# Two retention heads' values in seven half-size products instead of eight, in a TensorE-bound block

## The chip, the cores and the metric

The kernel runs on one core of a Trainium2 chip. The metric is the device time of one execution in microseconds (us). Inside the core, TensorE (PE in the profile, PEld for its weight loads) multiplies, VectorE (DVE) and ScalarE (ACT) do elementwise work, GpSimd (POOL) does small work and issues the DMAs of one queue, and SyncE (SP) issues the loads of the weights.

## The reference

Two layers of a block on 512 frames of width 1024. The part that matters here is the retention branch: one combined projection of the normalised input gives, among others, for each of four heads q and k (256 columns each), the values v (512 columns) and the gate g (512 columns).

```python
z = h @ w_in[i] + b_in[i]
_, _, mv, mo, mi, mf, rq, rk, rv, rg, gm, gr = split_cols(z)
...
hr = retention_chunkwise(to_chunks(rq4...), to_chunks(rk4...), to_chunks(rv.astype(f32), R_HEADS), log_gamma)
y_r = (jax.nn.silu(rg.astype(f32)) * head_layernorm(hr, r_norm_g[i], R_HEADS)).astype(dt)
merged = jax.nn.sigmoid(gm) * (y_m @ w_bm[i]) + jax.nn.sigmoid(gr) * (y_r @ w_br[i])
```

Everything is computed to float32 accuracy: each operand is split into a high and a low part (type fp32r), and each product is made of three matmuls, high·high, high·low and low·high.

## The kernel before, in words

**Units of weights.** All weights pass through the core once, as a written list of units (`unit_list`). A `T8` unit holds 1024 rows by 128 columns, gives one 128x512 output tile with the weights as the stationary operand, and takes 24 matmuls with 512 moving columns. A `V` unit holds 256 rows by 512 columns; four of them (`values`, L608 on) give the values of one head with the activations stationary and the weights moving, 96 matmuls of 512 columns. A `PAIR` unit gives two output tiles (256 columns) by a seven-product scheme (Winograd's form of Strassen's): quarters of the activations and sums of quarters (`sevenfold`, `xs`) times quarters of the weights B11, B12, B21, B22 and their sums t1 = B12+B11, t3 = B12+B22, t2 = t1+B22 and t4 = t2+B21 (the second output tile is carried with its sign turned, so all four are additions). That is 84 matmuls of 256 columns (`run_pair`, L421 to L423) instead of 48 of 512. Its last product P4 is put off (`later`) and run by `flush` inside the next unit.

**How a unit's weights come in.** SP loads each piece into one of four `wr` buffers (`fill_raws`, L341 and L343). ScalarE copies it into the high part and VectorE subtracts to get the low part (`split`, L263 and L264). Three such split pieces of 128x1024 are held at a time (`PIECES`). A `PAIR` has pieces A, B, C of 128x1024 (two blocks each) and D of 128x512 (t4). Loads and splits keep the order of the list; splits are asked for two pieces ahead (`LOOK`).

**The weight sums.** t1, t2, t3, t4 of each group of pairs are made in DRAM by DMAs that POOL issues: for each sum one copy and one accumulating copy of 1 MB (0.5 MB in the group `gm`), 8 steps a group, 20 groups, 160 steps (`step`, L307). `due(k)` gives the unit before which step k is issued; it also waits for the last matmul written so far. A group's steps are all issued before its first load.

**Order around the change.** In each layer: mLSTM heads, then `rv_vals(0)`, four tiles of the mLSTM output product, q and k of head 0, gates and four more tiles, then per head scores, attend, values and `r_out` (the gate projection as two pairs, and sixteen transposes, `back`). Values of head 1 come after attend of head 0, those of head 2 after q and k of head 2, those of head 3 after the eight `br` tiles. The framework's scheduler may interleave independent instructions of an engine; tiles of a tag (six `tmp` tiles, `qk`, `v`, eight PSUM banks) are handed out as they come free.

Of the kernel before, what the change touches and what calls it, by code (L numbers as in the profile page):

```python
# [35 lines left out]
F32 = mybir.dt.float32  # L36
# [58 lines left out]
MADE = {"t1": ("B12", "B11"), "t3": ("B12", "B22"), "t2": ("t1", "B22"), "t4": ("t2", "B21")}  # L95

READY = {"P1": 2, "P4": 2, "P5": 3, "P2": 4, "P6": 4, "P3": 4, "P7": 5}


def due(k):  # L100

    return 3 + 5 * min(k, 20) // 4 + 7 * max(k - 20, 0) // 4


def groups():


    g = {}
    for i in range(L):
# [12 lines left out]
        for b in range(4):  # L122
            g[i, f"ff{b}"] = [("w_ff2", b * 1024, 256 * p) for p in range(4)]
    return g


def unit_list(i):

    u = [("IF",)]

    def t8(w, col, row=0):
        u.append(("T8", w, row, col))

# [72 lines left out]
    pairs(ff_order()[0])  # L206
    u.append(("PE", 0))
    u.append(("PE", 1))
    pairs(ff_order()[1])
    full("w_pe_gate")  # L210
    return u


def build(ctx, tc, ins, out):
# [27 lines left out]
    br_dram = tc.dram_tile([L, KT, P, T], F32, name="br_spill")  # L242
    gm_dram = tc.dram_tile([L, 4, P, T], F32, name="gm_spill")
    bm_dram = tc.dram_tile([L, KT, P, T], F32, name="bm_spill")


    bc = cpool.tile([P, L, NB], F32, name="bc")
# [22 lines left out]
        cur[kind] = new  # L270


    index, given, sums, k = {}, {}, {}, 0
    for g, v in groups().items():
        index[g] = len(index)
        for x in GIVEN:
            given[g, x] = ins["wpairs"][k:k + len(v)]
            k += len(v)
        for x in MADE:
            sums[g, x] = tc.dram_tile([len(v), P, Q], F32, name=f"s{index[g]}{x}")  # L280

    def block(g, x):
        return given[g, x] if x in GIVEN else sums[g, x]
# [4 lines left out]
    def sum_steps():  # L288

        first = lambda g: [(g, "t1", 0), (g, "t3", 0), (g, "t1", 1), (g, "t3", 1)]  # L290
        second = lambda g: [(g, "t2", 0), (g, "t2", 1), (g, "t4", 0), (g, "t4", 1)]
        gs = list(index)
        out = first(gs[0])
        for a, b in zip(gs, gs[1:]):
            for x, y in zip(second(a), first(b)):
                out += [x, y]
        return out + second(gs[-1])

    steps = sum_steps()
# [2 lines left out]
    def step():  # L302
# [5 lines left out]

        tc.add_manual_dep(dma.ins, cur["mm"].ins.name, SYNC, reason="pace of the sums")

    def next_unit():
        n = at["unit"]
        at["unit"] += 1
        while at["step"] < len(steps) and due(at["step"]) <= n:
            step()
        return n


    order = [(n, x) for n, u in enumerate(units) for x in (PIECE if u[0] == "PAIR" else (0,))]
    place = {x: k for k, x in enumerate(order)}  # L320
    raws, pieces = {}, {}

    room = unit_list(0).index(("T8", "w_out", 0, 0))
    cur["room"], cur["more"] = (), None
    at = {"unit": 0, "prep": 0, "load": 0, "whole": 0, "step": 0}

    def fill_raws(most=RAWS + 1):
        while at["load"] < len(order) and len(raws) < most:
            n, x = order[at["load"]]
# [6 lines left out]
            raws[n, x] = r = r or wpool.tile([P, UN], F32, name=f"wr{at['load']}", tag="wr", bufs=RAWS)  # L336
            if x:
                _, g, p = units[n]
                assert made[g] == 8, (g, made[g], at["unit"])
                for k, y in enumerate(PIECE[x]):  # L340
                    in_order("load", nc.sync.dma_start(r[:, k * Q:(k + 1) * Q], block(g, y)[p]))  # L341
            else:
                in_order("load", nc.sync.dma_start(r, ins["wstream"][at["whole"]]))  # L343
                at["whole"] += 1
            at["load"] += 1

    def prep_next():
        n, x = order[at["prep"]]
        at["prep"] += 1
        fill_raws()  # L350

        w = Q if x == "D" else UN
        pl = cur["last"] if n >= NU - LAST else wpool
        kw = {"tag": "d", "bufs": 2} if x == "D" else {"tag": "l", "bufs": 2 * LAST} if pl is not wpool else {
            "tag": "w", "bufs": 2 * PIECES}
        out_ = [pl.tile([P, w], F32R, name=f"w{a}{n}_{x}", **kw) for a in "hl"]
# [45 lines left out]
    def run_pair(name, act, done):  # L402
# [31 lines left out]
        for x in ("P6", "P2", "P3", "P7"):  # L434
            product(x)
        later.append(last)

    def pair_tiles(name, act, consume, y=None):

# [350 lines left out]
    for i in range(L):  # L790
# [163 lines left out]
            head_scale(nm, num, 512, mv, hv)  # L954
            return num

        def r_out(h, num, y):
            nm = f"l{i}r{h}o"
            gs = {}

            def gates(w):
                def consume(g):
                    for d in range(2):
                        ac.activation(g[d], g[d], AF.Silu, bias=bcol(i, "brg", 4 * h + 2 * w + d), scale=SIGN[d])
                        gs[2 * w + d] = g[d]

                return consume

            for w in range(2):
                pair_tiles(f"{nm}{w}", xs, gates(w))  # L970
            for v in range(4):
                o = back(nm, num, v)
                if v == 0:
# [36 lines left out]
        def mv_vals(pr, act, rc, mid=None):  # L1010
            return values(i, f"l{i}m{pr}", act, rc, bias_rows(pr * 512), 2, mid)

        def rv_vals(h, mid=None):
# [93 lines left out]
        num = r_attend(2, pt, vv)  # L1107
        qk = r_qk(3)
        for c in range(KT):
# [231 lines left out]
    cur["last"].release()  # L1341
    n3_pool.release()
    x_pool.release()
    assert at["unit"] == NU and at["prep"] == len(order) and not pieces and not raws and at["load"] == len(order) and at["step"] == len(steps)

def _pack_units(a):
# [7 lines left out]
    for i in range(L):  # L1356
        for u in unit_list(i):
            if u[0] == "T8":
                _, nm, r, c = u
                put(a[nm][i, r:r + D, c:c + P])  # L1360
            elif u[0] == "PAIR":
                continue
            elif u[0] == "V":
                _, k, c = u
# [11 lines left out]

def _pack_pairs(a):

    out = []
    for (i, _), g in groups().items():  # L1380
# [3 lines left out]
    return np.ascontiguousarray(np.concatenate(out))  # L1384


def _pack_vecs(a):
# [70 lines left out]
```

## Time and profile before

| what | value |
|---|---|
| median of 3 runs | 2363.36 us (2362.84 to 2367.16) |
| span of the profiled execution | 2361.2 us |
| TensorE, matmuls | 2339.5 us busy, 13788 instructions |
| VectorE | 1579.5 us, 67% |
| ScalarE | 1194.3 us, 51% |
| GpSimd | 262.1 us, 11% |

The profile gives the profiled execution no time of its own beside the span; the runs lie 1.6 to 6.0 us above that span. Matmuls overlap in the pipeline, so one that is shown 389 ns long is followed by the next after about 227 ns: what a matmul costs is read from the distance between starts, not from its length.

### The profile page before, as it was taken

To read this page: it belongs to the slowest core of one execution; us is meant where nothing else is said; L and a number is where in the kernel's file an instruction comes from. 1 tells how busy PE (TensorE), PEld (TensorE's weight loads), DVE (VectorE), ACT (ScalarE), POOL (GpSimd) and SP (SyncE) were. 2 spreads that over 40 slices of the span, in tenths; PEclk is the share of its full clock that TensorE was granted. 3 is DMA by queue.
4 is the path that set the end of the run, shared out by engine and by line. 5 is a ranking of instruction groups with operands and counts; after the bars stand their busy time and mean duration, and the time that the engine had idled before them with its cause. 6 is when DMAs were issued, how large, how long until landed. Compare 5 with 4: busy or idle time off the path is not lost. (4 is left out here: it accounts for less than half of the span.)

```text
span 2361.2 us, 35588 instructions
## 1 busy us (share of the span) xinstructions
PE 2339.5 (99%) x13788; PEld 2074.1 (88%) x13788; DVE 1579.5 (67%) x2435; ACT 1194.3 (51%) x1736; POOL 262.1 (11%) x380
## 2 busy tenths in 40 slices
PE   9999999999999999999999999999999999999998
PEld 7888898998998898899888888999989988998997
DVE  6877566764665676667778675676737656676675
ACT  5755344553553545445457563444526445455454
POOL 4121100000001100001321111000000020000012
PEclk9999999999999999999999999999999999999999
DMA  7766876768688777777776668776786894543441
GB/s 243 196 187 183 232 240 193 206 191 243 190 263 278 213 232 209 216 227 196 201 212 169 191 179 235 233 197 200 189 253 186 274 265 118 166 140 118 154 153 53
DMA packets 177576, 473.49 MB, mean 201 GB/s; under 512 B 17520, under 2 KB 19952, under 8 KB 177408
## 3 DMA queue, kind: packets, MB, share of 16 engines
q1 hardware_dynamic: 118512, 280.25, 35.3%
q0 software_dynamic: 41472, 159.39, 29.1%
q10 hardware_dynamic: 17424, 31.59, 3.7%
q8 instruction: 108, 1.77, 0.3%
q14 instruction: 60, 0.49, 0.1%
HBM read 456.48 MB, written 174.06 MB: 267 GB/s over the span
## 5 line engine op out<-in xcount | busy, mean ns | idle before, releaser
L263 ACT ACTIVATE wh<-wr 128x1024 fp32r<-128x1024 f32 x254 | 268.1, 1057 | 386.7 <-issue 55.2
L264 DVE TENSOR_TENSOR wl<-wr,wh 128x1024 fp32r<-128x1024 f32 x254 | 311.1, 1225 | 148.0 <-ACT wh L263 143.1
L263 ACT ACTIVATE wh_C<-wr 128x1024 fp32r<-128x1024 f32 x76 | 80.5, 1059 | 132.6 <-PE l0bm L373 13.1
L263 ACT ACTIVATE wh_B<-wr 128x1024 fp32r<-128x1024 f32 x76 | 80.4, 1058 | 85.3 <-PE l1bm L373 5.8
L264 DVE TENSOR_TENSOR wl_B<-wr,wh_B 128x1024 fp32r<-128x1024 f32 x76 | 93.9, 1235 | 43.7 <-ACT wh_B L263 43.2
L263 ACT ACTIVATE wh_A<-wr 128x1024 fp32r<-128x1024 f32 x76 | 80.1, 1055 | 76.6 <-PE l1f L373 11.3
L264 DVE TENSOR_TENSOR wl_A<-wr,wh_A 128x1024 fp32r<-128x1024 f32 x76 | 92.9, 1222 | 32.6 <-ACT wh_A L263 31.1
L264 DVE TENSOR_TENSOR wl_C<-wr,wh_C 128x1024 fp32r<-128x1024 f32 x76 | 92.8, 1221 | 29.0 <-ACT wh_C L263 29.0
L372 PE MATMUL l1f<-l1n2h,wh 128*128 128x512 f32 x256 | 99.8, 390 | 0.0
L372 PE MATMUL l0f<-l0n2h,wh 128*128 128x512 f32 x256 | 99.8, 390 | 0.0
L374 PE MATMUL l0f<-l0n2h,wl 128*128 128x512 f32 x256 | 99.7, 389 | 0.0
L374 PE MATMUL l1f<-l1n2h,wl 128*128 128x512 f32 x256 | 99.6, 389 | 0.0
L373 PE MATMUL l1f<-l1n2l,wh 128*128 128x512 f32 x256 | 99.6, 389 | 0.0
L373 PE MATMUL l0f<-l0n2l,wh 128*128 128x512 f32 x256 | 99.6, 389 | 0.0
L263 ACT ACTIVATE wh_D<-wr 128x512 fp32r<-128x512 f32 x76 | 47.6, 627 | 86.0 <-issue 5.3
L264 DVE TENSOR_TENSOR wl_D<-wr,wh_D 128x512 fp32r<-128x512 f32 x76 | 52.1, 686 | 46.3 <-ACT wh_D L263 43.9
L374 PEld LDWEIGHTS l1f<-l1n2h,wl 128*128 128x128 f32 x256 | 48.1, 188 | 10.1
L374 PEld LDWEIGHTS l0f<-l0n2h,wl 128*128 128x128 f32 x256 | 48.0, 188 | 10.0
L373 PEld LDWEIGHTS l0f<-l0n2l,wh 128*128 128x128 f32 x256 | 48.1, 188 | 9.8
L373 PEld LDWEIGHTS l1f<-l1n2l,wh 128*128 128x128 f32 x256 | 48.1, 188 | 9.8
L372 PEld LDWEIGHTS l0f<-l0n2h,wh 128*128 128x128 f32 x256 | 48.1, 188 | 9.8
L372 PEld LDWEIGHTS l1f<-l1n2h,wh 128*128 128x128 f32 x256 | 48.1, 188 | 9.8
(5492 smaller groups left out, 8236.2 us busy)
## 6 DMA issues: line engine op xcount, KB each, us to landing
wr<-wstream SPq DMA_DIRECT2D x254, 512.0 KB, 4.8
wr<-wpairs SPq DMA_DIRECT2D x228, 256.0 KB, 3.7
s0t<-wpairs POOLq DMA_DIRECT2D x6, 1024.0 KB, 8.2
s2t<-wpairs POOLq DMA_DIRECT2D x6, 1024.0 KB, 9.3
s3t<-wpairs POOLq DMA_DIRECT2D x6, 1024.0 KB, 9.0
s4t<-wpairs POOLq DMA_DIRECT2D x6, 1024.0 KB, 9.4
s5t<-wpairs POOLq DMA_DIRECT2D x6, 1024.0 KB, 9.7
s6t<-wpairs POOLq DMA_DIRECT2D x6, 1024.0 KB, 9.0
```

What stands on the lines that cost most here:

```text
L263: a = ac.activation(hi_ap, src, AF.Copy)
L264: return a, ve.tensor_sub(lo_ap, src, hi_ap.bitcast(F32))
L372: te.matmul(o, sh, mh, start=first, stop=False)
L373: te.matmul(o, sh, ml, start=False, stop=False)
L374: cur["mm"] = te.matmul(o, sl, mh, start=False, stop=last)
```

## The change

The values of two retention heads (1024 columns) become one `WIDE` unit. It uses the seven-product scheme with the activation quarters as stationary operand (`xs`, in halves of 128 frames) and weight blocks of 512 rows by 512 columns as moving operand, 512 columns wide. Two WIDE units a layer replace sixteen V units. Each WIDE has 14 pieces (seven blocks in two halves), and counts as seven ticks of the pace of the sums. Seven results per frame tile are combined by VectorE out of PSUM; the first head's values are split at once, the second head's are written to DRAM (`rv_spill`, ScalarE's queue) and read back and split later (`rv_load`).

For the pairs, t4 is no longer made in DRAM and loaded: after piece B (B21 and t2) is split, VectorE adds its two halves in the `wr` buffer, which stays taken until D is split from it. The WIDE groups have eight sum steps, pair groups six. `due` is changed.

The values of heads 2 and 3 are computed before q and k of head 2, not after; the first gate pair of heads 0 and 1 (`r_gates(h, 0)`) runs ahead of the scores of the next head.

```diff
+WIDE = (("P1", "B11", 0), ("P5", "t1", 4), ("P6", "t2", 5), ("P2", "B21", 2), ("P7", "t3", 3), ("P3", "B22", 6),
+        ("P4", "t4", 1))
-PIECE = {"A": ("B11", "t1"), "B": ("B21", "t2"), "C": ("B22", "t3"), "D": ("t4",)}
+PIECE = {"A": ("B11", "t1"), "B": ("B21", "t2"), "C": ("B22", "t3"), "D": ()}
 def due(k):
-    return 3 + 5 * min(k, 20) // 4 + 7 * max(k - 20, 0) // 4
+    return 3 + 6 * min(k, 60) // 4 + 7 * max(k - 60, 0) // 4
...
+        g[i, "rv0"] = [("w_in", 0, CRV)]
+        g[i, "rv2"] = [("w_in", 0, CRV + 1024)]
...
-    v(CRV)
+    u.append(("WIDE", (i, "rv0"), 0))
...
-    v(CRV + 512)
     rg(0)
+    u.append(("WIDE", (i, "rv2"), 0))
     rqk(2)
-    v(CRV + 1024)
     rg(1)
     rqk(3)
     full("w_br")
-    v(CRV + 1536)
...
     (prep_next)
-        r = raws.pop((n, x))
+        r = raws.pop((n, "B" if x == "D" else x))
         in_order("prep", *split(r[:, :w], *out_))
         pieces[n, x] = out_
+        if x == "B":
+            ve.tensor_tensor(r[:, :Q], r[:, :Q], r[:, Q:], OP.add)
+            raws[n, x] = r
...
+    def run_wide(name, act, done, mid=None):
+        n = next_unit()
+        bank = {}
+        for at_, (x, y, j) in enumerate(WIDE):
+            if at_:
+                tick()
+            if x == "P6":
+                flush()
+            if x == "P2" and mid:
+                mid()
+            b = {"P2": "b", "P5": "c", "P3": "c"}.get(x, "a")
+            first = x in ("P1", "P2", "P5")
+            if first:
+                bank[b] = [ps(f"{name}{b}{t}") for t in range(2)]
+            for k in range(4):
+                if k % 2 == 0:
+                    ready(place[n, (y, k // 2)] + LOOK)
+                    wh, wl = pieces.pop((n, (y, k // 2)))
+                h, l = act[k](j)
+                s = slice(k % 2 * T, (k % 2 + 1) * T)
+                f, e = first and k == 0, k == 3
+                for t in range(2):
+                    ts = slice(t * P, (t + 1) * P)
+                    o = bank[b][t]
+                    te.matmul(o, h[:, ts], wh[:, s], start=f, stop=False, skip_group_check=True)
+                    te.matmul(o, h[:, ts], wl[:, s], start=False, stop=False, skip_group_check=True)
+                    cur["mm"] = te.matmul(o, l[:, ts], wh[:, s], start=False, stop=e, skip_group_check=True)
+            for t in range(2):
+                done(x, t, bank[b][t])
...
         def rv_vals(h, mid=None):
-            return values(i, f"l{i}r{h}", xn, None, bias_rows(1024 + h * 512), 1, mid)
+            nm = f"l{i}r{h}"
+            bv = [tmp(f"{nm}bv{d}") for d in range(2)]
+            for d in range(2):
+                nc.sync.dma_start(bv[d], bias_rows(1024 + (h + d) * 512))
+            y = [[cur["low"].tile([P, T], F32, name=f"{nm}y{d}{j}", tag="qk" + "hl"[d], bufs=4) for j in range(NT)]
+                 for d in range(2)]
+            v = value_tiles(nm)
+            def head0(j):
+                split(y[0][j], v[0][j][:, :T], v[1][j][:, :T])
+            def head1(j):
+                nc.scalar.dma_start(rv_dram[i, h // 2, j], y[1][j])
+            def done(x, t, o):
+                a, b = t, 2 + t
+                if x == "P1":
+                    ve.tensor_tensor(y[0][b], o, bv[0], OP.add)
+                elif x == "P2":
+                    ve.tensor_tensor(y[0][b], o, y[0][b], OP.add)
+                    head0(b)
...
+            run_wide(f"{nm}v", xs, done, mid)
+            return v
+        def rv_load(h):
+            v = value_tiles(f"l{i}r{h}")
+            for j in range(NT):
+                t = tmp(f"l{i}r{h}vr{j}")
+                nc.scalar.dma_start(t, rv_dram[i, h // 2, j])
+                split(t, v[0][j][:, :T], v[1][j][:, :T])
+            return v
...
         num = r_attend(0, pt, vv)
-        vv = rv_vals(1)
+        gs = {}
+        r_gates(0, 0, gs)
+        vv = rv_load(1)
         pt = r_scores(1, qk)
         yr = acts(cur["br"], f"l{i}yr0")
-        r_out(0, num, yr)
+        r_out(0, num, yr, gs)
         num = r_attend(1, pt, vv)
+        vv = rv_vals(2)
         qk = r_qk(2)
-        vv = rv_vals(2)
+        gs = {}
+        r_gates(1, 0, gs)
         pt = r_scores(2, qk)
-        r_out(1, num, yr)
+        r_out(1, num, yr, gs)
...
-        vv = rv_vals(3)
+        vv = rv_load(3)
```

More of the change, by code (lines that the diff above doesn't have):

```diff
@@ L270, in in_order @@
         cur[kind] = new
-    index, given, sums, k = {}, {}, {}, 0
+    index, given, sums = {}, {}, {}
+    at = {"unit": 0, "tick": 0, "prep": 0, "load": 0, "whole": 0, "step": 0, "wpairs": 0, "wwide": 0}
     for g, v in groups().items():
         index[g] = len(index)
+        src, n, w = ("wwide", 2, UN) if is_wide(g) else ("wpairs", len(v), Q)
         for x in GIVEN:
-            given[g, x] = ins["wpairs"][k:k + len(v)]
-            k += len(v)
+            given[g, x] = ins[src][at[src]:at[src] + n]
+            at[src] += n
         for x in MADE:
-            sums[g, x] = tc.dram_tile([len(v), P, Q], F32, name=f"s{index[g]}{x}")
+            if x != "t4" or is_wide(g):
+                sums[g, x] = tc.dram_tile([n, P, w], F32, name=f"s{index[g]}{x}")
     def block(g, x):
@@ L294, in sum_steps @@
         for a, b in zip(gs, gs[1:]):
-            for x, y in zip(second(a), first(b)):
-                out += [x, y]
+            s, f = second(a), first(b)
+            while s or f:
+                out += s[:1] + f[:4 // len(second(a)) if len(s) > 1 else 4]
+                f = f[4 // len(second(a)) if len(s) > 1 else 4:]
+                s = s[1:]
         return out + second(gs[-1])
@@ L309, in step, with tick @@
         tc.add_manual_dep(dma.ins, cur["mm"].ins.name, SYNC, reason="pace of the sums")
+    def tick():
+        while at["step"] < len(steps) and due(at["step"]) <= at["tick"]:
+            step()
+        at["tick"] += 1
     def next_unit():
@@ L313, in next_unit @@
         at["unit"] += 1
-        while at["step"] < len(steps) and due(at["step"]) <= n:
-            step()
+        tick()
         return n
-    order = [(n, x) for n, u in enumerate(units) for x in (PIECE if u[0] == "PAIR" else (0,))]
+    order = [(n, x) for n, u in enumerate(units) for x in parts_of(u)]
     place = {x: k for k, x in enumerate(order)}
+    loads = [(n, x) for n, x in order if x != "D"]
     raws, pieces = {}, {}
@@ L324, in build @@
     cur["room"], cur["more"] = (), None
-    at = {"unit": 0, "prep": 0, "load": 0, "whole": 0, "step": 0}
     def fill_raws(most=RAWS + 1):
-        while at["load"] < len(order) and len(raws) < most:
-            n, x = order[at["load"]]
+        while at["load"] < len(loads) and len(raws) < most:
+            n, x = loads[at["load"]]
             r = None
@@ L955, in r_attend, with r_gates, consume, r_out @@
             return num
-        def r_out(h, num, y):
-            nm = f"l{i}r{h}o"
[L959 to L970, printed above, removed]
+        def r_gates(h, w, gs):
+            def consume(g):
+                for d in range(2):
+                    ac.activation(g[d], g[d], AF.Silu, bias=bcol(i, "brg", 4 * h + 2 * w + d), scale=SIGN[d])
+                    gs[2 * w + d] = g[d]
+            pair_tiles(f"l{i}r{h}o{w}", xs, consume)
+        def r_out(h, num, y, gs=None):
+            nm = f"l{i}r{h}o"
+            if gs is None:
+                gs = {}
+                r_gates(h, 0, gs)
+            r_gates(h, 1, gs)
             for v in range(4):
@@ L1343, in build @@
     x_pool.release()
-    assert at["unit"] == NU and at["prep"] == len(order) and not pieces and not raws and at["load"] == len(order) and at["step"] == len(steps)
+    assert at["unit"] == NU and at["prep"] == len(order) and not pieces and not raws and at["load"] == len(loads) and at["step"] == len(steps)
 def _pack_units(a):
@@ L1360, in _pack_units @@
                 put(a[nm][i, r:r + D, c:c + P])
-            elif u[0] == "PAIR":
+            elif u[0] in ("PAIR", "WIDE"):
                 continue
@@ L1377, in _pack_pairs @@
 def _pack_pairs(a):
-    out = []
-    for (i, _), g in groups().items():
+    out, wide = [], []
+    for (i, nm), g in groups().items():
+        if is_wide((i, nm)):
+            (n, r, c), = g
+            w = a[n][i, r:r + D, c:c + 2 * T].reshape(2, 2, 2, P, 2, T)
+            b = {(k, m): w[:, :, k, :, m].transpose(0, 2, 1, 3).reshape(2, P, UN) for k in range(2) for m in range(2)}
+            wide += [b[int(x[1]) - 1, int(x[2]) - 1] for x in GIVEN]
+            continue
         w = np.stack([a[n][i, r:r + D, c:c + 2 * P].reshape(4, 2, P, 2, P) for n, r, c in g])
```

48 lines of the change are left out of this document (41 added, 7 removed).

## The prediction

> **What bounds the kernel now.** I read the page first, then the waits of TensorE, then single tiles for the distance between matmuls, then stretches where the change puts its work.
>
> ```profile
> span 2361.2 us, 35588 instructions
> ...
> PE 2339.5 (99%) x13788; PEld 2074.1 (88%) x13788; DVE 1579.5 (67%) x2435; ACT 1194.3 (51%) x1736; POOL 262.1 (11%) x380
> ...
> q1 hardware_dynamic: 118512, 280.25, 35.3%
> q0 software_dynamic: 41472, 159.39, 29.1%
> q10 hardware_dynamic: 17424, 31.59, 3.7%
> ...
> L263 ACT ACTIVATE wh<-wr 128x1024 fp32r<-128x1024 f32 x254 | 268.1, 1057 | 386.7 <-issue 55.2
> L264 DVE TENSOR_TENSOR wl<-wr,wh 128x1024 fp32r<-128x1024 f32 x254 | 311.1, 1225 | 148.0 <-ACT wh L263 143.1
> ...
> L264 DVE TENSOR_TENSOR wl_D<-wr,wh_D 128x512 fp32r<-128x512 f32 x76 | 52.1, 686 | 46.3 <-ACT wh_D L263 43.9
> ...
> wr<-wstream SPq DMA_DIRECT2D x254, 512.0 KB, 4.8
> ```
> ```profile
> PE l1bgm L374 <- DVE wl L264: 2.0, 1, 2.0
> PE l0o33a L421 <- DVE l0x L1211: 1.6, 1, 1.6
> PE l1o33a L421 <- DVE l1x L1211: 1.6, 1, 1.6
> ...
> PE l0o11a L421 <- DVE l0x L1211: 1.5, 1, 1.5
> ```
>
> TensorE is without work for 2361.2 - 2339.5 = 21.7 us of the whole span, and its named waits are a dozen of at most 2 us. Other engines have room on average. So the time is the sum of what TensorE streams, and a matmul removed is time removed, as long as the engines behind it still deliver in the stages that get denser. The price of a matmul is the distance between starts. The next rows are the tile of head 1's values in layer 0 (columns: count, duration in ns, first and last start):
>
> ```profile
> L624 PE MATMUL l0r1vp<-wh,l0xnh x32: 389/389/389, 387.8 to 408.9; 128*128 128x512 f32 x32
> ...
> L592 DVE TENSOR_TENSOR l0r1v<-l0r1vp,l0r1bv x4: 684/690/691, 407.8 to 410.9; 128x512 f32<-128x512 f32 x4
> ```
> ```profile
> 383.22 0.27 PE L421 MATMUL l0r1brka<-l0xnh,wh_D 128*128 128x256 f32 x1
> ...
> 384.64 0.40 PE L373 MATMUL l0r0a<-l0r0vl,l0r0ph 128*128 128x512 f32 x1
> ```
>
> L624 is every third matmul, so 31 x 3 = 93 distances take 408.9 - 387.8 = 21.1 us: 0.227 us each, though each is drawn 389 ns long. The twelve 256-column matmuls of a pair's P4 take 384.64 - 383.22 = 1.42 us, 0.118 each. A V or T8 unit (24 matmuls) is thus 5.45 us, a pair (84) 9.9 us.
>
> **The change, part by part.**
>
> *Matmuls.* Eight heads' values were 8 x 96 = 768 matmuls of 512 columns. Four WIDE units are 4 x 7 x 4 x 2 x 3 = 672, of the same shape: 128x128 stationary, split weights moving. 96 fewer at 0.227: **-21.8 us**. No row shows another distance for such an instruction, so I take no other price. The Trainium skill, in TensorE: Matmul & The Clock Gate, section Back-to-back issue gap, gives about 131 ns a matmul as the sustained figure for 512 columns; by that the 96 would be worth an estimated 12.6 us. The trace disagrees with that figure (0.227 us over 93 distances), and the measurement decides.
>
> *Splits of weights.* WIDE has 14 pieces for two heads, V had 8: 24 more splits, 24 x 1.057 = 25.4 us of ScalarE and 24 x 1.225 = 29.4 us of VectorE. *Combining:* 14 PSUM operations a WIDE at 0.69 instead of 8: 24 x 0.69 = 16.6 us of VectorE. *t4 in SBUF:* 76 additions of 128x512; the nearest row is wl_D, also two SBUF operands: 76 x 0.69 = 52 us. VectorE goes to 1579.5 + 98 = 1678 us, 72% of some 2345; ScalarE to 1220 us, 52%. None becomes the bound on average; the dense places decide.
>
> *Inside a WIDE.* Seven products of 5.45 us, 38.1 us. VectorE: 14 x 1.225 + 14 x 0.69 + 4 x 0.69 (splits of head 0) = 29.6 us, 78%; in `rv_vals(0)` the last mLSTM head's two tiles come on top, about 3 us, 86%. Stretches as full as this exist and cost TensorE nothing:
>
> ```profile
> 335.00:385.00 50.00, 50.00 (x349) 46.86 (x348) 30.42 (x46) 23.24 (x37) 2.70 (x3) 1.00 0.87 242
> 700.00:740.00 40.00, 40.00 (x252) 36.18 (x252) 24.21 (x33) 17.73 (x26) 2.37 (x3) 1.00 0.93 292
> 410.00:440.00 30.00, 30.00 (x228) 28.79 (x228) 24.02 (x38) 21.32 (x36) 0.94 (x1) 1.00 0.63 176
> 2245.00:2300.00 55.00, 52.98 (x396) 49.76 (x395) 43.07 (x58) 31.67 (x43) 6.89 (x5) 1.00 0.49 154
> ```
>
> (Stretch and length, then busy time of PE, PEld, DVE, ACT, POOL; clock; DMA share; GB/s.) In 410 to 440 VectorE is 24.02 of 30 us busy, 80%, and PE 30.00 of 30. P6 must wait until P1's PSUM tiles are read, but P5 lies between, 5.45 us for two reads of 0.69; in a pair it is 1.42 us. I cost these at 0.
>
> *DMA inside a WIDE: the open price.* A piece lasts 12 matmuls, 2.72 us, and brings 0.524 MB: 193 GB/s, where V and T8 ask for 96 and a pair for 1.83 MB in 9.9 us, 185. A sum step of 1.05 MB comes every 1.5 ticks, 8.2 us (1.75 ticks, 9.5 us, after step 60): 110 to 128 GB/s. Head 1's values go out, 1.05 MB in 38 us: 28. Demand: about 340 GB/s. What 16 engines gave with both kinds of traffic: 242 / 0.87 = 278 and 292 / 0.93 = 314 GB/s. Short by 26 to 62 GB/s, 1.0 to 2.4 MB per WIDE. It can fall on the sums, which nobody waits for at once, or on the loads. A load may take long: its buffer frees when piece j-4 is split, some 2.4 us after piece j-7 has left TensorE, and it must be split again before piece j starts: 6 x 2.72 - 4.8 = 11.5 us, against 4.8 us median on the page and 8.1 in the crowded 700 to 740:
>
> ```profile
> wr<-wstream SPq DMA_DIRECT2D x8, 512.0 KB, 8.1
> ```
>
> From below: 0, the sums lag. From above: all of it on the loads, 2.4 MB / 193 GB/s = 12.4 us less 11.5 - 8.1 = 3.4 us of slack, 9 us a WIDE. Shared half and half it is 2.6 to 6.2 us of lag against 3.4 of slack, 0 to 2.8. I take 1 us a WIDE, **+4 us**, near the lower end: in 335 to 385 pairs, with pieces nearly as short, ran at 87% DMA and PE did not wait once. Both ends, 0 and 36, are kept.
>
> *Sums.* 160 steps become 152: 20 groups lose two, four groups of eight come. Total DMA stays about equal: q1 loses 32 + 38 loads of 0.52 MB and gains 56, q10 gains 8.4 MB. The tightest deadline I count from the list is `rqk2` of layer 0: its last t2 step is due at tick 64, 21.8 us into the second WIDE, and its first load comes at tick 67, its t2 half is used 41 us after that WIDE began. The list before had nine ticks there (52 and 61). POOL waits in order, so a late sum holds what is behind it:
>
> ```profile
> POOL s5t L307 <- DMA s4t<-s4t: 9.4, 2, 4.8
> ```
>
> Two waits, 9.4 us in all; no wait of TensorE names them. 21.8 + 10 for the copy, + 4 load, + 2.4 split = 38 us: met, by 3 us. 0, inside the DMA range.
>
> *D from SBUF.* Where VectorE is itself the end, an addition is path. That is the last four pairs of a layer, 2245 to 2300 above (PE 52.98 of 55):
>
> ```profile
> 2287.24 1.21 DVE L264 TENSOR_TENSOR wl_B<-wr,wh_B 128x1024 fp32r<-128x1024 f32 x1
> 2288.37 0.41 DVE L1211 TENSOR_TENSOR l1x<-l1x,l1o32a 128x256 f32<-128x256 f32 x1
> 2288.70 1.21 DVE L264 TENSOR_TENSOR wl_C<-wr,wh_C 128x1024 fp32r<-128x1024 f32 x1
> ```
>
> No gap between them, and TensorE waits for those L1211. Two pairs a layer on path: 4 x 0.6 = **+2.4 us**; from below 0, from above all eight, 5.5. In the other 68 pairs the addition sits behind B's split and before C's; D is needed last, so 0, as VectorE has a third of its time free; the 1.5 us wait of l0o11a says that now and then it does not. The 76 loads that fall away on SP free nothing TensorE waits for: 0.
>
> *Moves.* The gate pair ahead of the scores keeps two of six `tmp` tiles for longer, while `rv_load` wants four and the scores four. The nearest row for a read-back on ScalarE's queue:
>
> ```profile
> l0gml<-gm_spill ACTq DMA_DIRECT2D x4, 256.0 KB, 4.8
> ```
>
> 4.8 us, then 4 x (0.63 + 0.69) of splits, within the gate pair's 9.9; the values are used a scores stage, a pair and sixteen transposes later, over 15 us. From attend to `back` there remain a gate pair, the scores (3.8 us) and another pair, 24 us, for some 8 us of statistics on VectorE and POOL. 0, at most 2 a head, and a gain as large if waits dissolve. The two bias loads on SP wait for `tmp` tiles that are free since the scores; loads of later pieces stand behind them: 0.
>
> **Sum.** 2361.2 - 21.8 + 4 + 2.4 = 2345.8 us of span. The runs' median is 2.2 us above the span (2363.36), so 2348.0. Measurement can tell about 0.2%, 4.7 us, from no change.
>
> **The rivals.**
>
> *Slower: WIDE starves.* If loads take the whole shortage, and TensorE waits 6 us or more per WIDE, four waits eat -21.8 + 2.4 and go past it; the upper bound, 9 us, gives +36 instead of +4: 2380. A wait costs more than itself, as layer 1's start shows:
>
> ```profile
> 1283.89 0.50 PE L374 MATMUL l1bgm<-l1n1h,wl 128*128 128x512 f32 x1 [1.96 <-DVE wl L264]
> ...
> 1284.94 0.63 PE L372 MATMUL l1bgm<-l1n1h,wh 128*128 128x512 f32 x1
> 1285.36 0.63 PE L373 MATMUL l1bgm<-l1n1l,wh 128*128 128x512 f32 x1
> ```
>
> After 1.96 us without work, matmuls start 0.42 us apart for about eight of them, 1.6 us more. For it: 340 GB/s against 278 to 314. Against it: 335 to 385 and 700 to 740 with PE full. The Trainium skill, in DMA: Bandwidth & Descriptors, section Issuing engines are not separate DMA queues, says that transfers started by ScalarE, SyncE and GpSimd share the same 16 engines and interleave, which speaks for the shortage reaching the loads; the trace agrees in so far as the loads land in 8.1 us where all three are active, against 4.8. Chance 0.12.
>
> *Most of the gain eaten.* 3 to 5 us per WIDE, with VectorE's additions in other pairs: 2357 to 2366. Chance 0.14.
>
> *The full gain and more.* The DMA shortage falls on the sums, the additions fall into gaps, and one or two old waits go with the new order: 2363.4 - 21.8 - 3 = 2338. Chance 0.10.
>
> *The matmuls are not shorter in number where it counts,* because WIDE's start to start is longer than 0.227 (PSUM written in pairs of banks, activations from other tiles): at 0.26 the gain is gone, 672 x 0.26 = 174.7 against 768 x 0.227 = 174.3. No tile of the trace shows it. It is within the 0.12.
>
> **How the numbers follow.** The forecast, 2340 to 2356, 0.64. Range 2338 to 2365. Faster by over 0.2%: 0.64 + 0.10 + about 0.08 of the eaten case = 0.82; within 0.2%: 0.06; slower: 0.12.
>
> **What would show it.** The WIDE tiles 0.227 us apart, 13692 matmuls, L624 to L626 left only for the mLSTM values; PE busy near 2320 at 99%. VectorE near 1678 us. Loads of WIDE pieces landing in 6 to 10 us, and PE waits named after `rv` tiles summing below 5 us; over 20 us of these, or matmuls 0.42 apart in them, and I am wrong. In the last pairs of a layer, waits for L1211's successor 2 to 3 us longer in all.

## The result, and the profile after

The changed kernel takes 2371.47 us (median of 6 runs, 2367.79 to 2373.87) against 2364.44 us for the kernel before (6 runs beside it). The ratio is 1.0026, with a 95% interval of 1.0016 to 1.0037. It is slower by about a quarter of a per cent, where a gain of 15 us was forecast, and it lies outside the range of 2338 to 2365.

First the page of the changed kernel: the span, the busy time of each engine, two of its DMA queues (q1, which brings the weights, and q10, which carries the spills; packets, MB, share), and the landing time of the WIDE loads.

```profile
span 2366.1 us, 35463 instructions
...
PE 2330.3 (98%) x13692; PEld 2063.0 (87%) x13692; DVE 1665.7 (70%) x2559; ACT 1215.6 (51%) x1760; POOL 261.9 (11%) x372
...
q1 hardware_dynamic: 111024, 272.90, 33.9%
...
q10 hardware_dynamic: 22032, 39.98, 4.7%
...
wr<-wwide SPq DMA_DIRECT2D x24, 512.0 KB, 5.0
```

The 96 matmuls are gone (13788 to 13692) and VectorE and ScalarE are as busy as forecast. But TensorE is busy for only 9.2 us less (2339.5 to 2330.3), and it stands without work for 2366.1 - 2330.3 = 35.8 us instead of 21.7. So 14.1 us of new idle time came, and of the 21.8 us of matmuls removed some 12.6 us were given back by matmuls that run further apart.

The waits of TensorE in the changed kernel say where (what waited, for whom; us in all, times, the longest):

```profile
PE l0r2brqa L460 <- ACT l0r2brqy L516: 7.0, 1, 7.0
PE l0wo L411 <- ACT l0mh L284: 2.5, 1, 2.5
PE l0r2o1a L460 <- ACT wh_A L284: 2.3, 1, 2.3
PE l1r2o1a L460 <- ACT wh_A L284: 2.2, 1, 2.2
PE l1o33a L460 <- DVE l1x L1337: 2.0, 2, 1.5
PE l0o33a L460 <- DVE l0x L1337: 2.0, 2, 1.5
...
PE l0r0o0a L460 <- DVE l0r0o0y L526: 1.1, 1, 1.1
PE l1r0o0a L460 <- DVE l1r0o0y L526: 1.1, 1, 1.1
```

The first four and the last two were not in the list before. No tile of a WIDE (they are named `l0r0va` to `l1r2vc`) is there. The loss lies outside the new unit: in q of head 2 of layer 0 (`l0r2brq`), in the gates of head 2 of both layers (`l0r2o1`, `l1r2o1`), at the start of the output product of layer 0 (`l0wo`) and in the gates of head 0.

A wait costs more than its own length. These are stretches of the changed kernel around the first of them (length, then busy time of PE, PEld, DVE, ACT, POOL, granted clock, DMA share, GB/s):

```profile
478.00:489.00 11.00, 4.35 (x31) 3.91 (x29) 4.53 (x6) 3.65 (x6) 0.00 (x0) 0.80 1.00 231
489.00:494.00 5.00, 4.66 (x22) 4.66 (x23) 2.75 (x4) 2.00 (x5) 0.90 (x1) 0.50 1.03 310
494.00:500.00 6.00, 6.00 (x49) 6.00 (x49) 4.14 (x6) 2.50 (x3) 0.00 (x0) 0.93 1.05 271
```

After the wait of 7.0 us the granted clock is 0.50 in 489 to 494, and matmuls of 256 columns start 0.21 us apart instead of 0.118. The Trainium skill, in TensorE: Matmul & The Clock Gate, section Part 1: The HAM clock gate (the "warmup" mystery), says that an idle window of about 3.4 us brings the array to half its rate and that about as long a busy stretch releases it. The 0.50 behind a wait of 7.0 us agrees; the release came later here, since the matmuls start 0.21 us apart from 489.34 to 494.85, for 5.5 us.

To get the whole balance I added up the distances between the starts of successive matmuls. At their undisturbed values (0.227 us with 512 columns, 0.118 with 256) the matmuls of the kernel before make 2323.5 us and those of the changed kernel 2301.6 us, 21.8 us less, as forecast. What lies above these values grew from 29.1 to 56.1 us, by 27.0:

| place | added us |
|---|---|
| `l0r2brq`: the wait of 7.0 and the slow matmuls behind it | 9.5 |
| gates of head 2, `r2o0` and `r2o1`, two layers | 6.5 |
| gates of head 0, `r0o0` and `r0o1`, two layers | 4 |
| `l0wo` | 3.3 |
| WIDE's own matmuls, longer distance | 2.4 |
| last pairs of a layer (`o33`) | 0.9 |
| `l1bgm` and `l0o11`, shorter waits | -5.5 |

These make 21.1; the other 6 are spread over many smaller places. The experiments take the large rows one by one.

**The first row, step by step.** I name the chain from its start. First, GpSimd's DMAs in layer 0 (start, length, and what ended the idle time before it):

```profile
441.09 0.67 POOL L334 DMA_DIRECT2D s5t<-s5t  x1 [28.21 <-PE l0r1a L413]
446.58 0.65 POOL L334 DMA_DIRECT2D s6t<-wpairs  x1 [2.84 <-PE l0r2va L505]
457.73 0.56 POOL L334 DMA_DIRECT2D s6t<-wpairs  x1 [10.50 <-PE l0r2va L505]
463.27 0.97 POOL L334 DMA_DIRECT2D s5t<-wpairs  x1 [4.98 <-PE l0r2vb L505]
```

`s5t` holds the sums of q and k of head 2 (`rqk2`), `s6t` those of the group after it. The second WIDE of layer 0 starts at 440.3. The accumulating step that finishes t2 of `rqk2` is issued at 463.27, 23.0 us later, behind two steps of a group that is needed later. The next row is the landing time of that step, from the DMA issues of 440 to 485, and then SyncE's loads:

```profile
s5t<-wpairs POOLq DMA_DIRECT2D x1, 1024.0 KB, 12.3
```
```profile
464.99 0.33 SPq L375 DMA_DIRECT2D wr<-wpairs  x1
475.56 0.32 SPq L375 DMA_DIRECT2D wr<-s5t  x1
```

The sum lands 12.3 us after its issue. SyncE reaches the load of that t2 right after 464.99 and stands there until 475.56; every load behind it in the list, piece C of this pair among them, is issued after that. Now ScalarE and then TensorE:

```profile
480.74 1.06 ACT L284 ACTIVATE wh_B<-wr 128x1024 fp32r<-128x1024 f32 x1 [5.79 <-issue]
486.41 1.06 ACT L284 ACTIVATE wh_C<-wr 128x1024 fp32r<-128x1024 f32 x1 [4.61 <-DMA wr<-s5t]
...
488.93 0.36 ACT L516 ACTIVATE l0r2brqy<-l0r2brqa 128x256 f32<-128x256 f32 x1
```
```profile
489.34 0.58 PE L460 MATMUL l0r2brqa<-l0xsh,wh_B 128*128 128x256 f32 x1 [7.00 <-ACT l0r2brqy L516]
```

The matmul of 489.34 has its weights: wh_B was there at 481.8. It waits for its PSUM tile, which ScalarE empties in order behind the split of piece C, and that split waited for a load that had stood behind the late sum. The load of piece C was held for some 10 us and then took another 10 us to land (issued at 475.97 and 476.44, split at 486.41), beside the loads, a sum step and spills that went out within the same few us. The late block itself cost little; what stood behind it in two queues cost the 7 us.

### The profile page after: what moved, and what is told of

The parts are those of the page before. It is cut to its first block, busy times and chain, and to the rows that moved or that the text cites. A ratio compares the mean times of both kernels' runs of the same rounds, so it can differ in the third digit from the quotient of the medians.

```text
span 2366.1 us, 35463 instructions
## 1 busy us (share of the span) xinstructions
PE 2330.3 (98%) x13692; PEld 2063.0 (87%) x13692; DVE 1665.7 (70%) x2559; ACT 1215.6 (51%) x1760; POOL 261.9 (11%) x372
## 3 DMA queue, kind: packets, MB, share of 16 engines
q8 instruction: 107, 1.75, 0.3%
## 5 line engine op out<-in xcount | busy, mean ns | idle before, releaser
L284 ACT ACTIVATE wh<-wr 128x1024 fp32r<-128x1024 f32 x222 | 234.3, 1057 | 318.5 <-issue 70.6
L285 DVE TENSOR_TENSOR wl<-wr,wh 128x1024 fp32r<-128x1024 f32 x222 | 272.0, 1226 | 102.9 <-ACT wh L284 101.9
L284 ACT ACTIVATE wh_B<-wr 128x1024 fp32r<-128x1024 f32 x100 | 105.8, 1058 | 111.0 <-issue 20.6
L285 DVE TENSOR_TENSOR wl_B<-wr,wh_B 128x1024 fp32r<-128x1024 f32 x100 | 122.2, 1222 | 45.0 <-ACT wh_B L284 43.8
L285 DVE TENSOR_TENSOR wl_C<-wr,wh_C 128x1024 fp32r<-128x1024 f32 x76 | 92.7, 1220 | 25.0 <-ACT wh_C L284 25.0
L284 ACT ACTIVATE wh_t<-wr 128x1024 fp32r<-128x1024 f32 x32 | 34.0, 1062 | 50.3 <-PE l1r2va L504 7.0
```

The source lines that it names most:

```text
L284: a = ac.activation(hi_ap, src, AF.Copy)
L285: return a, ve.tensor_sub(lo_ap, src, hi_ap.bitcast(F32))
```

## The experiments

The edits are to the changed kernel, where nothing else is said. Times are compared by ratios to the kernel before on the same chip; 0.001 of the ratio is 2.4 us, and a difference of two ratios is uncertain by about 3 us.

**The late sum.** The steps of t2 of `rqk2` of layer 0 are issued before the first steps of the next group, not between them.

```diff
             s, f = second(a), first(b)
+            if a == (0, "rqk2"):
+                out += s
+                s = []
+                out += f
+                f = []
```

> The changed kernel, with the two t2 steps of the pairs after the second WIDE unit of layer 0 issued ahead of the next group's four first steps (ticks 60 and 61 instead of 60 and 64); nothing else. Theory 1 (a late weight sum): TensorE's wait of 7.0 us at l0r2brqa goes, and with it the about 2 us of slow matmuls behind it; 9 us less than the changed kernel's 2371.5, about 2362, ratio to before 0.999. Theory 2 (the DMA engines are short of bandwidth around a WIDE, whatever the order): the wait moves to loads of wr, at least 5 us of it stay, ratio 1.001 to 1.003.

Measured: 2362.56 us, ratio 0.9988 (0.9979 to 0.9997), 0.0038 or 9 us below the changed kernel. The step is now issued at 447.25; GpSimd's DMAs and the first rows of the waits of TensorE in this kernel:

```profile
447.25 0.99 POOL L339 DMA_DIRECT2D s5t<-wpairs  x1 [3.19 <-DMA s5t<-s5t]
```
```profile
PE l1r2o1a L465 <- ACT wh_A L284: 2.7, 1, 2.7
PE l0wo L416 <- ACT l0mh L284: 2.6, 1, 2.6
```

The wait of `l0r2brqa` is gone from the list. One DMA of GpSimd, issued 16 us earlier (and two steps of the next group some 12 and 6 us later), undoes the largest row of the table.

**The read-back.** Next the gates of head 2. ScalarE in the changed kernel, in layer 1:

```profile
1779.92 0.63 ACT L284 ACTIVATE l1r3vh<-l1r3vr 128x512 fp32r<-128x512 f32 x1 [1.25 <-DMA l1r3vr<-rv_spill]
...
1782.43 1.04 ACT L284 ACTIVATE wh_A<-wr 128x1024 fp32r<-128x1024 f32 x1
1783.37 0.36 ACT L516 ACTIVATE l1r2o0y<-l1r2o0a 128x256 f32<-128x256 f32 x1
```

The row of 1779.92 is the third of four splits of head 3's values as they come back from DRAM; the two before it waited for their landings in the same way, 4.1 us together with this one, and the fourth follows without a wait. The split of the next pair's piece A and the emptying of PSUM come behind them. The edit moves the read-back ahead of the eight `br` tiles.

```diff
+        vv = rv_load(3)
         for c in range(KT):
             o = t8(yr, f"l{i}br0{c}")
...
-        vv = rv_load(3)
```

> The changed kernel, with the read-back of head 3's values written ahead of the eight br tiles instead of behind them; nothing else. Theory (ScalarE stands in order behind the read-back while the next pair's weights and PSUM tiles wait): the waits of 2.3 and 2.2 us at l0r2o1a and l1r2o1a and the slow matmuls behind them go, 5 to 7 us less than 2371.5, about 2365.5, ratio 1.0004. Rival (these pairs are late because VectorE is full there): waits of the same size stay at r2o1a, ratio 1.0026.

Measured: 2363.86 us, ratio 0.9987 (0.9978 to 0.9997), 9 us below the changed kernel by the medians, though its profiled span, 2364.0, is only 2.1 us shorter than the other. In the distances between starts the gates of head 2 lose their 6.5 us, but `l0wo` grows from 3.3 to 5.9 us; the runs spread over 8 us, and the size is less sure than the mechanism. ScalarE here:

```profile
1778.44 0.39 ACT L516 ACTIVATE l1r2o0y<-l1r2o0a 128x256 f32<-128x256 f32 x1 [1.21 <-PE l1r2o0a L462]
...
1779.74 1.06 ACT L284 ACTIVATE wh_A<-wr 128x1024 fp32r<-128x1024 f32 x1 [0.71 <-PE l1r2o0c L461]
```

ScalarE now waits for TensorE there, and the waits of `r2o1a` are gone from the list in both layers. The four splits run some 40 us earlier (1731 to 1743), where ScalarE waits 8.4 us for their landings, and no wait of TensorE follows them there.

**Both together.**

> The changed kernel with both edits, the t2 steps ahead in layer 0 and the early read-back of head 3. If the two costs are separate they add: 9 us and 9 us (what the two runs gave by their medians' ratios) off 2371.5, ratio 0.995. If one wait hides behind the other, the sum is not reached: ratio 0.9985 as with one alone.

Measured: 2356.06 us, ratio 0.9958 (0.9942 to 0.9973), 16 us below the changed kernel against 18 for the sum of the two. What is left at the head of its list of waits is a place that neither edit touches:

```profile
PE l0wo L416 <- ACT l0mh L284: 3.0, 1, 3.0
```

**The start of `wo`, and the pace of the sums.** In the changed kernel that place looks as follows: GpSimd, then a row of the DMA issues of 715 to 757, then ScalarE.

```profile
722.23 0.90 POOL L334 DMA_DIRECT2D s9t<-wpairs  x1 [14.55 <-PE l0br L413]
730.28 0.90 POOL L334 DMA_DIRECT2D s9t<-wpairs  x1 [7.15 <-PE l0gr3c L462]
```
```profile
l0bml<-bm_spill ACTq DMA_DIRECT2D x3, 256.0 KB, 15.1
```
```profile
745.18 0.38 ACT L528 ACTIVATE l0gr3y<-l0gr3a 128x256 f32<-128x256 f32 x1 [7.82 <-DMA wr<-wstream]
```

Two sum steps fall 8 us apart beside the read-back of the merge; a 256 KB read takes 15.1 us, and ScalarE stands idle for 7.8 us. The view puts this down to a load of weights, though the row itself empties a PSUM tile; between its work ScalarE's queue also issues loads of the residual, so which transfer held it is not shown. The next edit adds to both others a slower pace: after step 60, two ticks a step instead of 1.75.

```diff
-    return 3 + 6 * min(k, 60) // 4 + 7 * max(k - 60, 0) // 4
+    return 3 + 6 * min(k, 60) // 4 + 8 * max(k - 60, 0) // 4
```

> Both edits, and after step 60 a sum step every two ticks instead of 1.75. Theory (the wait of 2.5 us at l0wo is a load of weights that shares the full DMA engines with two sum steps): that wait shrinks or goes, 2 to 4 us less than with both edits alone. Rival (the residual and spill loads fill the engines there by themselves): l0wo stays at 2.5 us, same time as with both edits.

Measured: 2349.61 us, ratio 0.9928 (0.9914 to 0.9941), 7 us below the two edits alone and faster than both kernels. That is more than the 2 to 4 us of the theory, which counted little beyond the wait: in the distances between starts `l0wo` cost 5.4 us with both edits, wait and slow matmuls together, and nothing here. The page and the first waits of this version:

```profile
span 2348.1 us, 35478 instructions
```
```profile
PE l1o33a L465 <- DVE l1x L1342: 2.0, 2, 1.5
PE l0o33a L465 <- DVE l0x L1342: 1.9, 2, 1.5
```

`l0wo` no longer waits, and what heads the list is what headed it before the change. So the whole change, with three places outside the seven products mended, is worth some 17 us (0.0072 of 2364) against the kernel before; by the two profiled spans it is 13.1 us.

**Is it the pace alone?** Two runs ask for that: the slower pace in the changed kernel without the other edits, and the same in the kernel before, for its steps from 60 on:

```diff
-    return 3 + 5 * min(k, 20) // 4 + 7 * max(k - 20, 0) // 4
+    return 3 + 5 * min(k, 20) // 4 + 7 * min(max(k - 20, 0), 40) // 4 + 8 * max(k - 60, 0) // 4
```

> The changed kernel with the slower pace of the sums after step 60 alone (every two ticks), t2 order and read-back as in the changed kernel. If the three costs are separate: 6 us less than 2371.5 (what the pace gave on top of the other two edits), the waits at l0r2brqa (7 us) and r2o1a (2.3 us) stay, l0wo goes; ratio 1.000. If the pace works only together with the other edits: ratio 1.0026.

> The kernel before with the slower pace after step 60 alone. Theory (the cost is two sum steps that fall into the full stretch before l0wo in the changed kernel, the kernel before has no wait there): no change within 2 us, ratio 1.000. Rival (a slower pace is better everywhere, and the gain of the repaired kernel is not the products'): 5 us faster, ratio 0.998.

The changed kernel with the slower pace takes 2365.94 us, ratio 1.0008 (0.9999 to 1.0017), 4 us below the changed kernel, between the two expectations and nearer to separate costs. `l0wo` is gone from its waits, and they keep the other two causes of above:

```profile
PE l0r2brqa L460 <- ACT l0r2brqy L516: 5.5, 1, 5.5
PE l1r2o1a L460 <- ACT wh_A L284: 3.0, 1, 3.0
```

The kernel before with the slower pace takes 2371.25 us, ratio 1.0028 (1.0017 to 1.0040): slower by 6.7 us, which I expected under no theory. A slower pace is not better everywhere. It moves the sums against the loads, and what it gives differs from version to version. With both edits and the old pace the change is already 10 us faster than the kernel before (0.9958), so the gain of the mended version does not come from the pace alone. Whether the kernel before would gain from some other pace or order was not tried, so the 17 us are against that kernel as it stood.

**The additions in SBUF.** Two runs price them. In the first, the kernel before gets only this part of the change: t4 by VectorE, six sum steps a group, no load of D.

```diff
-PIECE = {"A": ("B11", "t1"), "B": ("B21", "t2"), "C": ("B22", "t3"), "D": ("t4",)}
+PIECE = {"A": ("B11", "t1"), "B": ("B21", "t2"), "C": ("B22", "t3"), "D": ()}
...
+        if x == "B":
+            ve.tensor_tensor(r[:, :Q], r[:, :Q], r[:, Q:], OP.add)
+            raws[n, x] = r
```

> The kernel before with only the pairs' t4 made by VectorE in SBUF: no t4 steps, no loads of D, values in V units as before, old pace. By the prediction's term: 2 to 3 us slower (0 to 5.5), waits only in the last pairs of a layer, ratio 1.001. Rival a (52 us more of VectorE cost in many pairs): 8 us or more, ratio 1.0035. Rival b (relief of the DMA engines by 76 loads and 40 steps gains something): ratio 0.999.

Measured: 2367.96 us, ratio 1.0008 (0.9999 to 1.0016), 1.9 us. Its waits show the ends of the layers 0.4 and 0.3 us longer than the 1.6 of the kernel before, and `l1bgm` at 3.3 us where it was 2.0:

```profile
PE l1bgm L380 <- DVE wl L264: 3.3, 1, 3.3
PE l0o33a L427 <- DVE l0x L1217: 2.0, 2, 1.5
PE l1o33a L427 <- DVE l1x L1217: 1.9, 2, 1.5
```

In the distances between starts the last four pairs of the two layers (`o30` to `o33`) take 2.0 us more, which is the prediction's term, but two of the other groups of four (`o0`, `o2`) take 3.7 us more as well, and the third (`o1`) 0.6 us less. The median agrees with the term; the places do so in part.

In the second, the changed kernel loses the 76 additions and nothing else.

```diff
         if x == "B":
-            ve.tensor_tensor(r[:, :Q], r[:, :Q], r[:, Q:], OP.add)
             raws[n, x] = r
```

> The changed kernel without VectorE's 76 additions: D is split from B21 alone, so the fourth product of every pair is computed from a wrong block; all else is the same. It prices the additions in the denser schedule. By the prediction's term 2 to 3 us (the kernel before with the additions alone: 1.9 us by the median): ratio 1.0015. Rival (in the retention stage the additions are what makes VectorE late): 5 us or more off 2371.5, and the waits at r0o0a, r0o1a go: ratio 1.0005 or less.

Measured: 2367.50 us, ratio 1.0004 (0.9993 to 1.0015), 5 us below the changed kernel (3.6 by the spans). Its waits:

```profile
PE l0r2brqa L459 <- ACT l0r2brqy L515: 4.7, 1, 4.7
PE l0wo L410 <- ACT l0mh L284: 2.4, 1, 2.4
PE l1r2o1a L459 <- ACT wh_A L284: 1.8, 1, 1.8
PE l0r2o1a L459 <- ACT wh_A L284: 1.7, 1, 1.7
```

Every place that waits is still there, shorter by up to 2.3 us. The additions cause none of the three places; the waits are shorter without them. The time is that of the rival, but the waits at `r0o0a`, which the rival wanted gone, are still 1.1 us; with some 3 us of uncertainty, 5 us cannot be told from the 2 to 3 of the term. That an addition lies on a chain of splits that is late already is a reading, not a test.

**The gates that run ahead.** The edit takes the two early gate pairs of a layer back to their old place.

```diff
-        gs = {}
-        r_gates(0, 0, gs)
         vv = rv_load(1)
...
-        r_out(0, num, yr, gs)
+        r_out(0, num, yr)
...
-        gs = {}
-        r_gates(1, 0, gs)
         pt = r_scores(2, qk)
-        r_out(1, num, yr, gs)
+        r_out(1, num, yr)
```

> The changed kernel with both gate pairs of heads 0 and 1 back inside r_out, as in the kernel before. Theory (the gate pair ahead crowds VectorE and ScalarE beside rope, statistics and read-back, which gives the 1.1 us waits at r0o0a and 0.5 at r0o1a in both layers): 3 to 5 us less than 2371.5, ratio 1.001. Rival (the gate pair hides the chain from attend over the statistics to the transposes, which is short now that no values stand between): waits of TensorE on l0r0num or l0r0ot appear, 4 us or more slower than 2371.5, ratio 1.0045.

Measured: 2395.74 us, ratio 1.0126 (1.0112 to 1.0141), 24 us above the changed kernel. The new waits:

```profile
PE l0r2s L411 <- ACT l0r2kh L284: 4.5, 1, 4.5
PE l1r2s L411 <- ACT l1r2kh L284: 4.5, 1, 4.5
PE l0r2brka L460 <- DVE l0r2brky L526: 3.4, 1, 3.4
```

The rival had the direction, with a ratio of 1.0045 instead of 1.0126, and named another place: no wait appears on `l0r0num` or `l0r0ot`. With the values of heads 2 and 3 ahead of q and k of head 2, nothing stands between k and the scores that need it; the gate pair fills that place. The scores of head 1 wait too (`r1s`, 1.9 us in each layer), where the values of head 1 stood before. The gate pair belongs to the move of the WIDE and is not an extra.

**The gates of head 0.** The 1.1 us waits of `r0o0a` stood in every version with the gate pair ahead, and the read-back of head 1 stands just ahead of them. So it was moved behind the scores, on top of the first two edits.

```diff
-        vv = rv_load(1)
         pt = r_scores(1, qk)
+        vv = rv_load(1)
```

> Both edits, and the read-back of head 1 written behind the scores of head 1. Theory (the 1.1 us waits at r0o0a come from the read-back's splits between the gate pair's and the scores' work): they go, 2 to 4 us less than with both edits. Rival (VectorE is full there by rope, statistics and the addition whatever comes in between): the waits stay within 0.5 us, same time.

Measured: 2361.49 us, ratio 0.9982 (0.9973 to 0.9991), 6 us above the same kernel without this edit. The waits of `r0o0a` stay at 1.1 us, and a new one comes:

```profile
PE l1r1a L416 <- ACT l1r1vh L284: 2.2, 1, 2.2
```

The read-back is not what holds `r0o0a`. In the changed kernel VectorE, for which it waits, is busy for 5.00 of the 5 us from 417 to 422, where TensorE is busy for 3.89. Without the additions the wait is 1.1 us as well. Which of VectorE's other instructions could go elsewhere was not tried, so this row of the table stays open.

**WIDE's longer distance.** Two rows, one of each of two tiles of the same WIDE in the changed kernel, give the distance (count, duration in ns, first and last start; every third matmul, so 21 distances lie between first and last):

```profile
L503 PE MATMUL l0r2va<-wh_B,l0xnh x8: 389/389/389, 440.6 to 445.3; 128*128 128x512 f32 x8
```
```profile
L503 PE MATMUL l0r2vc<-wh_t,l0xsh x8: 393/396/398, 446.0 to 450.9; 128*128 128x512 f32 x8
```

4.7 and 4.9 us over 21 distances; from the unrounded starts it is 0.227 with the quarters of the activations (`xn`) as stationary operand and 0.233 with the sums (`xs`). Over the four WIDEs that makes 672 matmuls in 155.4 us, against 768 in 174.5 before. The last run moves the `xs` tiles in SBUF by 64 bytes a partition, on top of the mended version.

```diff
+        xs_pool.tile([P, 16], F32, name="shift2", tag="shift2")
         shift(xs_pool, act_side, True)
```

> The kernel with both edits and the slower pace, and the tiles of the activation sums moved by 64 bytes a partition in SBUF; nothing else. In the WIDE units the matmuls with a sum as stationary operand start 233 ns apart, those with a plain quarter 227. Theory (the address of the stationary tile against that of the moving weights sets it): the 233 changes, to 227 or to something else, at most 2.4 us (384 x 6 ns). Rival (it belongs to the product, not to the address): 233 stays. Time within 3 us of the kernel without the shift, ratio 0.9928.

Measured: 2349.15 us, ratio 0.9929 (0.9909 to 0.9948), no difference to 2349.61. The same tile as above in this kernel:

```profile
L508 PE MATMUL l0r2vc<-wh_t,l0xsh x8: 393/396/398, 445.8 to 450.7; 128*128 128x512 f32 x8
```

From the unrounded starts the mean distance with the sums is 0.2335 us in layer 0, as before the move, and 0.2325 in layer 1, where it was 0.2335. The place in SBUF, by this step, is not it, and the cause stays open. It is worth 2.4 us.

## Why the prediction was wrong, point by point

- **The sums: the step that failed.** It read "38 us: met, by 3 us. 0, inside the DMA range" for `rqk2` of layer 0. The place was right, and the times were close: 23.0 us to the issue where I had 21.8, 12.3 for the landing where I had 10. These 3.5 us ate the margin of 3. But the price was not the overrun. I asked when the one block would be there, and not what stands behind its load on SyncE and behind its neighbour's split on ScalarE. The cost was 9.5 us in the trace and 9 us by the run that undoes it: the step failed in its price of 0 for a deadline met so closely. I had also let the missing bandwidth fall on the sums, "which nobody waits for at once", as the cheap case, in the same text in which one sum had 3 us of slack: the two steps contradicted each other.
- **The moves: 0, mis-sized.** I costed the splits of the read-back against the time at which the values are used, over 15 us later, and found cover. They are not late; they are early in ScalarE's order, and the 4 us for which they wait for DMA hold the weights and the PSUM tiles of others. Price: 6.5 us by the trace, 9 by the medians. The bound of 2 us a head was too low (6.5 us for one read-back in each of two layers): the splits that it rested on were busy times, without the waiting for the landings.
- **A place that I did not look at.** `l0wo`, 3.3 us by this trace, 5.4 by that of both edits, and 7 by the run with the other pace. My DMA argument covered the WIDEs alone, but `due` is changed for the whole list. In 700 to 740, the crowded stretch that I quoted for comfort, the kernel before issued steps at 707, 720 and 735, the changed one at 701, 707, 722 and 730.
- **Matmuls: -21.8 in number, -19.1 in time.** The distance in a WIDE averages 0.231 us and not 0.227. "No row shows another distance" held for the kernel before only; the rival of a longer distance was right in kind, at about an eighth of the size that decides.
- **DMA inside a WIDE: +4, measured 0.** No WIDE tile waits. The stretch of the first WIDE of layer 0 in the changed kernel:

```profile
250.00:295.00 45.00, 44.88 (x205) 36.77 (x204) 35.52 (x54) 21.35 (x26) 6.14 (x9) 1.00 0.98 322
```

  The DMA engines moved 322 GB/s at a share of 0.98, above the 278 to 314 that I took for their limit (those stretches were not full), the WIDE loads landed in 5.0 us, and TensorE was busy for 44.88 of 45 us. So the price of a lag inside the unit was not there. That the shortage fell on the sums instead is not shown: the sum that was late at `rqk2` landed 2.3 us later than supposed, in a stretch (440 to 485) with a DMA share of 0.81.
- **D from SBUF: +2.4.** Right in size in the kernel before: 1.9 us by the medians (-0.2 to 3.8), and 2.0 us in the trace at the pairs where I put it. The 0 for the other 68 pairs was not right: there the trace has 3.7 us more at `o0` and `o2`, and 0.6 less at `o1`. In the changed kernel the additions cost 5, with some 3 us of uncertainty.
- **Gate pairs ahead, 0.** Not quite: `r0o0` and `r0o1` take 4 us more in the table, and why is open. But the place itself is right; without the pairs ahead it is 24 us more.
- **The forecast of engine loads** was right for VectorE (1665.7 us of 1678), ScalarE (1215.6 of 1220), the 8.4 MB more of spills on q10 and the 13692 matmuls, and was no help: none of the losses shows in these totals. TensorE was busy for 2330.3 us where near 2320 was forecast, and the WIDE loads landed in 5.0 us instead of 6 to 10. The sign was wrong through three engines whose work is done in order (GpSimd's steps, SyncE's loads, ScalarE's splits), none of which is near its limit over the whole span. The rival for "slower", WIDE starving, was the wrong mechanism at the wrong place.

The mended version ends at 2349.61 us, near the 2348.0 that was forecast for the change as it stood. That is not a confirmation: its balance has other terms (19.1 us of matmuls, some 2 to 5 of additions) and a pace that the change does not have.

## What to carry to other kernels

When a change makes a transfer or an operation later, price not only the thing that is late but everything behind it on each engine that works in order: a load that waits for a sum holds the next loads, a split that waits for a load holds the emptying of PSUM, and that is what TensorE feels. A deadline met by 3 us, with a landing time that can vary by as much (9.7 us as the median, 12.3 here), is not a cost of 0 but a chance of the whole queue's delay. Place a read-back where its engine has room to wait, not merely early enough for its reader; and take up the pace of background transfers afresh after a change, since the same step of pace gave 7 us in one version and cost 7 in another.

## What the runs showed of the hardware that was not expected

- The same matmul (128x128 stationary, 512 moving columns) has starts 0.227 us apart with one set of tiles as stationary operand and 0.233 with another; a move of the second set by 64 bytes a partition left it at 0.2335 in one layer and 0.2325 in the other. The cause is open.
- Beside copies and accumulating copies inside DRAM, 322 GB/s were moved over 45 us at a DMA share of 0.98, more than in the stretches of the kernel before that the prediction shows (292 at 0.93). In slices of about one us it is up to 419 GB/s within 715 to 757 of the changed kernel, and up to 422 within 700 to 740 of the kernel before, whose mean of 292 includes slices of 0 to 20. So a mean over a stretch that is not full is no limit. Nor does a full share fix the rate: 478 to 489 has 231 GB/s at 1.00. Why it differs was not tried.
- A wait of 2.2 us (`l1r2o1a`) was followed by matmuls at the full clock, while a wait of 1.96 us in the kernel before was followed by a granted clock of 0.66 over the next 5 us. The length of a wait alone does not tell what follows it.
